# Both heads in one DRAM transfer, copies made by the fetch, and a block sum spread over the first pair: a change to a two-layer hybrid decoder trunk

## The chip, the cores and the metric

The kernel runs on one core of one Trainium2 chip. Its time is the device time of one execution in microseconds (us). The median of three runs of the kernel before is 2662.35 us (2662.26 to 2664.25). A core has five engines that run side by side, each with its own in-order stream of instructions: TensorE (PE, matrix products; the load of its weights is shown as PEld), VectorE (DVE), ScalarE (ACT), GpSimd (POOL) and SyncE (SP). In this kernel SP computes nothing: nearly all DMA transfers are issued from its queue, one after the other, and a transfer whose condition is not met holds back all that are queued behind it.

## The reference, cut to what matters

The input has 1024 tokens with 1024 features. There are two layers, each a pair of attention mixers with gates and then a gated convolutional FFN:

```python
h = rmsnorm(x, norm1[l])
proj = h @ w_in[l]                       # q, k, v of both mixers and the gates
o_a = dilated_mixture(qa, ka, va)        # 3 groups x 4 heads: windows 128/512/2048, dilation 1/4/16
o_b = stick_breaking_attention(qb, kb, vb)   # 4 heads
g_a, g_b = sigmoid gates of proj
x = x + (g_a * (o_a @ w_br[l, :OUT_A]) + g_b * (o_b @ w_br[l, OUT_A:])) @ w_o[l]
h2 = rmsnorm(x, norm2[l])
a, v = h2 @ w_up[l]
x = x + (gelu(causal_depthwise_conv(a)) * v) @ w_down[l]
```

A head has 64 features. The result must have float32 accuracy: the kernel writes every operand of a product as a rounded high part plus a low part and sums three matrix products (high by high, low by high, high by low), so that each product costs three passes of PE.

## The kernel before, in words

**Products in seven instead of eight.** The large projections go in *pairs*: two column blocks of 128 of `w_in` by the two halves of the tokens and the two halves of the features, a 2x2 block product that is done with seven block products instead of eight (`pair`, L1055). The price is in sums of blocks of the weights (L1077, L1078 on POOL, then on DVE) and of blocks of `h`. The four sums of `h` are called S[1] to S[4]; each has four parts of 128 features. They are made by `block_sums` (L984) in small pieces that stand in the list `dense.side`; the last is `fourth` (L1010): per part three additions of 128x512 on DVE (L1014 to L1016), then `split` (L136), that is, one copy on ACT for the high part and one subtraction on DVE for the low part. S[4] is written in place over the first block of `h` and is read by the seventh product of a pair alone.

**The order of PE.** PE's order is written by hand. The class `Dense` (L220) hands out the dense work in small steps; one step is six matrix products of 128x512 or so. First come four *plain* products (gates, L1211), then the pairs. `attend` (L361) walks over the attention items and asks for dense steps between their small pieces with `advance`; each call also does one piece of `dense.side`. When the first pair is to begin, what is left of `dense.side` is done at once (L310 to L315). `dense.at(n, f)` does `f` n steps later. The order on ACT, DVE, POOL and SP is set by a scheduler from the order of the program and the priorities in it.

**The items of a layer.** B0 to B15 are stick-breaking items (`stick_item`), N00 to N11 the near group of the dilated mixer (window 128, `near_item`, with ACT exponentials at L774 and the application of the weights at L796), T00 to T17 the two far groups together (`far_item`). A far item is one head pair `pr`, one head `s` of the pair and one remainder `r` of four. Pairs that are needed by an item come before it: `pair_near` for keys and queries of the stick-breaking and near heads, `pair_v` for values, `pair_kq` for keys and queries of the far groups (one pair for each group and head pair: four in a layer).

**The way through DRAM.** Results of these pairs go through DRAM to change their layout. A pair has four results (column block c, token half n); `put` writes each.

- `pair_kq.put` (L1139) writes keys and queries to `tk`. The high part of a key goes to rows 0 to 63 and the low part to rows 64 to 127; the high part of a query is written twice, to both row halves, and its low part once. Each of these is written for each of the two heads of the pair by a transfer of its own: 4 for a key block and 6 for a query block, 20 for a pair, each 64 rows by 4 remainders by 128 columns (L1148). The quarter that stays zero is written once by `zeros` (L1046) in the first layer.
- `fetch_kq` (L835) reads for one far item all six blocks of 128 rows by 256 with one transfer, into a new buffer (tag `xa`, four buffers for everything of that tag).
- `values_part` (L545) writes the values of the first four heads to `sv`, one transfer for a head (L566). `pair_v`'s `turn` (L1172) writes all other values, one transfer for each of two heads (L1186). The tiles hold the heads inside a token row (`j h c`, `r h c`).
- `fetch_row`, `fetch_values`, `fetch_whole` and `fetch_v` read stick-breaking and near keys, queries and values; they write into `slots` and `kv`.

The weights of the pairs come from `in_w_in_dram` (L1069), two transfers for a pair, on the same queue.

Of the kernel before, what the change touches and what calls it, by code (L numbers as in the profile page):

```python
# [7 lines left out]
F32 = mybir.dt.float32  # L8
# [54 lines left out]
def trunk_kernel(ctx, tc, x, norm1, w_in, b_gate, w_br, w_o, norm2, w_up, conv_w, conv_b, w_down, norm_f, out, depth=None, probe=None):  # L63
# [52 lines left out]
    tk = [dr.tile([2, 4, P, 6, 256], F32, name=f"tk{i}") for i in range(2)]  # L116
# [3 lines left out]
    sv = [dr.tile([P, KD, P], F32, name=f"sv{i}") for i in range(8)]  # L120
# [99 lines left out]
    class Dense:  # L220
# [324 lines left out]
    def values_part(vt, w, ms):  # L545
        for m in ms:
# [12 lines left out]
            ov = o.rearrange("p (j h c) -> p j h c", j=2, h=4)  # L559
            vv = vt[m // 2][:, 2 * (m % 2) : 2 * (m % 2) + 2, :, :]  # L560
# [95 lines left out]
    def fetch_values(j):  # L656
        u, qp = j // 4, 3 - j % 4
        t = slice(256 * qp, 256 * qp + 256)
        nc.sync.dma_start(f32(R["kv"][:, 1, t]).rearrange("p (b c) -> p b c", c=P), sv[u][:, 2 * qp : 2 * qp + 2, :])

    def fetch_whole(v):
# [6 lines left out]
        nc.sync.dma_start(f32(kv[:, 1, :]).rearrange("p (b c) -> p b c", c=P), sv[4 + v])  # L668
# [166 lines left out]
    def fetch_kq(i):  # L835

        t = R["kq", i] = sb.tile([P, 6, 256], F32R, tag="xa", bufs=4, name="t_kq")
        nc.sync.dma_start(f32(t), tk[i // 8][i // 4 % 2, i % 4])
# [5 lines left out]
    def far_item(dense, pr, s, r, share):  # L844
# [8 lines left out]
        def score():  # L853
# [7 lines left out]
            t = R["kq", i]  # L861
            for g in range(2):
                scores(z0[:, P * g : P * g + P], t[:, 3 * g + 1, 0:P], t[:, 3 * g + 2, 0:P], t[:, 3 * g, 0:P])
            for g in range(2):
                scores(z1[:, 256 * g : 256 * g + 256], t[:, 3 * g + 1, P:256], t[:, 3 * g + 2, P:256], t[:, 3 * g, :])
# [118 lines left out]
    def block_sums(more):  # L984
# [56 lines left out]
        todo += more  # L1041
        for i in range(4):
            todo.append(({"plain"}, lambda i=i: fourth(i)))
        return todo

    def zeros():  # L1046

        none = sb.tile([P, 4, 256], F32, tag="ot", name="none")
        pool.memset(none[0:64], 0.0)
        for pr in range(2):  # L1050
            for g in range(2):
                for s in range(2):
                    nc.sync.dma_start(tk[pr][s, :, 64:128, 3 * g + 2, :].rearrange("r p c -> p r c"), none[0:64])
# [82 lines left out]
    def pair_kq(dense, l, g, pr):  # L1136
        off = 256 * g + P * pr

        def put(c, n, x, psum, room=None):  # L1139
# [4 lines left out]
            for s in range(2):  # L1144
                rows = slice(64 * s, 64 * s + 64)
                for src, kind, up in ((hv, c, 0), (hv, 1, 64), (lv, 2, 0)) if c else ((hv, 0, 0), (lv, 0, 64)):
                    there = tk[pr][s, :, up : up + 64, 3 * (g - 1) + kind, n * P : (n + 1) * P]
                    nc.sync.dma_start(there.rearrange("r p j -> p r j"), f32(src[rows]))  # L1148
# [20 lines left out]
    def pair_v(dense, l, g):  # L1169


        def turn(c, n, f):  # L1172
# [4 lines left out]
            vv = sb.tile([P, 4, 2, P], F32R, tag="ot", name="vv")  # L1177
            with tc.high_priority(offset=AHEAD):
                act.copy(vv[:, :, :, 0:64], tw)
                dve.tensor_tensor(vv[:, :, :, 64:128], tw, f32(vv[:, :, :, 0:64]), ALU.subtract)  # L1180
            for h in range(2):
                if g:
                    there = tv[c][h, :, :, g - 1, n * P : (n + 1) * P].rearrange("r p c -> p r c")
                else:
                    there = sv[4 + 2 * c + h][:, 4 * n : 4 * n + 4, :]
                nc.sync.dma_start(there, f32(vv[:, :, h, :]))  # L1186
# [46 lines left out]
    def mixer(l, pending):  # L1233
# [6 lines left out]
        dense.side = block_sums([(set(), zeros)] * (l == 0))  # L1240
# [850 lines left out]
```

## Time and profile before

| what | value |
|---|---|
| median of 3 runs | 2662.35 us |
| profiled execution, its time | 2664.07 us |
| profiled execution, its span | 2662.4 us |
| mean granted TensorE clock | 0.997 |
| PE busy | 2628.7 us, 99% of the span |
| DVE, ACT, POOL busy | 78%, 50%, 28% |
| DMA | 478.76 MB, 416103 packets, mean 180 GB/s |

The span runs from the first to the last instruction. PE is busy nearly always, so whatever shortens the kernel without taking work from PE must be in the hundredth of the span in which PE stands still, or in stretches in which PE runs with a reduced clock. Busy times of the other engines are averages over stages with different limits. A view of stretches gives for each stretch its length, then the busy time of PE, PEld, DVE, ACT and POOL in it (with the number of instructions), the granted clock as a share of the full one, the share of the 16 DMA engines that was busy and GB/s. A view of waits gives the engine and line that waited, what ended the wait, the us in total, how often, and the longest.

### The profile page before, as it was taken

To read this page: it belongs to the slowest core of one execution; us is meant where nothing else is said; L and a number is where in the kernel's file an instruction comes from. 1 tells how busy PE (TensorE), PEld (TensorE's weight loads), DVE (VectorE), ACT (ScalarE), POOL (GpSimd) and SP (SyncE) were. 2 spreads that over 40 slices of the span, in tenths; PEclk is the share of its full clock that TensorE was granted. 3 is DMA by queue.
4 is the path that set the end of the run, shared out by engine and by line. 5 is a ranking of instruction groups with operands and counts; after the bars stand their busy time and mean duration, and the time that the engine had idled before them with its cause. 6 is when DMAs were issued, how large, how long until landed. Compare 5 with 4: busy or idle time off the path is not lost.

```text
span 2662.4 us, 36856 instructions
## 1 busy us (share of the span) xinstructions
PE 2628.7 (99%) x12780; PEld 2195.4 (82%) x12780; DVE 2070.3 (78%) x3094; ACT 1338.6 (50%) x2488; POOL 733.9 (28%) x609
## 2 busy tenths in 40 slices
PE   9999999999999999999999999999999999999999
PEld 8788878888888888888888888788888888888888
DVE  5887867785888888897659777567958888898865
ACT  5555556564545554432435555565645455554225
POOL 5422201121233443321162221101321343344210
PEclk9999999999999999999999999999999999999999
DMA  8443578773243544588442445886632544446863
GB/s 262 140 140 113 159 195 234 239 262 103 80 150 135 174 141 157 221 320 320 154 156 97 140 135 157 203 246 223 229 101 71 180 140 152 148 168 248 334 247 119
DMA packets 416103, 478.76 MB, mean 180 GB/s; under 512 B 25652, under 2 KB 335276, under 8 KB 414124
## 3 DMA queue, kind: packets, MB, share of 16 engines
q1 hardware_dynamic: 415900, 476.39, 55.0%
q8 instruction: 101, 1.65, 0.3%
q14 instruction: 86, 0.70, 0.1%
q10 hardware_dynamic: 16, 0.00, 0.0%
HBM read 307.43 MB, written 168.89 MB: 179 GB/s over the span
## 4 chain that ended last, share of the span: by engine, by line
PE 80%; DVE 10%; DMA 4%; ACT 2%; issue 2%; SPq 1%; POOL 1%; DVEq 0%; ACTq 0%; POOLq 0%
PE u_a L978 5%; PE u_a L980 5%; PE u_a L979 5%; PE d_ps L1719 5%; PE d_ps L1721 4%; PE d_ps L1720 4%; PE i_a L978 4%; PE i_a L980 3%; PE i_a L979 3%; PE u_c L979 3%; PE u_c L980 3%; PE u_c L978 3%; PE o_ps L181 2%; PE o_ps L180 2%; PE o_ps L182 2%
## 5 line engine op out<-in xcount | busy, mean ns | idle before, releaser
L146 DVE TENSOR_TENSOR w_lo<-up_a,w_hi 128x512 fp32r<-128x512 f32 x240 | 237.4, 996 | 20.5 <-ACT w_hi L139 20.5
L139 ACT CAST w_hi<-up_a 128x512 fp32r<-128x512 f32 x240 | 149.3, 622 | 184.1 <-PE u_a L979 45.4
L1727 DVE TENSOR_TENSOR x<-x,d_ps 128x512 f32<-128x512 f32 (+1 forms) x228 | 152.0, 671 | 78.4 <-PE d_ps L1721 77.0
L1458 POOL TENSOR_TENSOR cv<-cv 128x512 f32<-128x512 f32 x88 | 132.3, 1516 | 249.6 <-DVE cv L1453 139.7
L139 ACT CAST w_hi<-in_a 128x512 fp32r<-128x512 f32 x192 | 119.2, 621 | 130.5 <-PE i_c L979 45.9
L146 DVE TENSOR_TENSOR w_lo<-in_a,w_hi 128x512 fp32r<-128x512 f32 x192 | 142.5, 742 | 38.7 <-ACT w_hi L139 32.4
L146 DVE TENSOR_TENSOR g<-cv,g 128x512 fp32r<-128x512 f32 x154 | 151.9, 988 | 5.2 <-ACT g L139 2.7
L1077 POOL TENSOR_TENSOR u<-in_a 128x512 f32<-128x512 f32 x32 | 45.7, 1428 | 364.2 <-DMA in_a<-in_w_in_dram 116.2
L1719 PE MATMUL d_ps<-gd_in,w_hi 128*128 128x512 f32 (+1 forms) x340 | 130.3, 383 | 1.4 <-ACT w_hi L139 0.6
L1721 PE MATMUL d_ps<-gd_in,w_lo 128*128 128x512 f32 (+1 forms) x340 | 129.8, 382 | 0.0
L1720 PE MATMUL d_ps<-gd_in,w_hi 128*128 128x512 f32 (+1 forms) x340 | 129.7, 382 | 0.0
L978 PE MATMUL u_a<-hh,w_hi 128*128 128x512 f32 x320 | 124.7, 390 | 0.8 <-DVE u L1609 0.8
L980 PE MATMUL u_a<-hh,w_lo 128*128 128x512 f32 x320 | 124.5, 389 | 0.0
L979 PE MATMUL u_a<-hl,w_hi 128*128 128x512 f32 x320 | 124.5, 389 | 0.0
L980 PE MATMUL u_a<-t_hi,w_lo 128*128 128x512 f32 x320 | 124.5, 389 | 0.0
L979 PE MATMUL u_a<-t_lo,w_hi 128*128 128x512 f32 x320 | 124.5, 389 | 0.0
L978 PE MATMUL u_a<-t_hi,w_hi 128*128 128x512 f32 x320 | 124.5, 389 | 0.0
L146 DVE TENSOR_TENSOR w_lo<-w_raw,w_hi 128x512 fp32r<-128x512 f32 x96 | 77.0, 804 | 58.6 <-ACT w_hi L139 51.7
L691 POOL TENSOR_SCALAR_AFFINE_SELECT beta<-beta 128x128 f32<-128x128 f32 x64 | 31.8, 497 | 306.3 <-ACT beta L687 306.3
L139 ACT CAST g<-cv 128x512 fp32r<-128x512 f32 x154 | 95.0, 617 | 40.1 <-POOL cv L1458 29.6
L1719 PE MATMUL d_ps<-gd_in,wd 128*128 128x512 f32 (+1 forms) x292 | 113.9, 390 | 0.0
L1721 PE MATMUL d_ps<-gd_in,wd 128*128 128x512 f32 (+1 forms) x292 | 112.8, 386 | 0.0
(395 smaller groups left out, 8651.1 us busy)
## 6 DMA issues: line engine op xcount, KB each, us to landing
gd<-g SPq DMA_DIRECT2D x154, 512.0 KB, 3.6
gd_in<-gd SPq DMA_DIRECT2D x154, 512.0 KB, 6.8
up_a<-in_w_up_dram SPq DMA_DIRECT2D x80, 512.0 KB, 5.6
in_a<-in_w_in_dram SPq DMA_DIRECT2D x64, 512.0 KB, 5.6
t_kq<-tk SPq DMA_DIRECT2D x32, 768.0 KB, 4.9
wd_raw<-in_w_down_dram SPq DMA_DIRECT2D x22, 1024.0 KB, 11.7
gin<-gs SPq DMA_DIRECT2D x32, 512.0 KB, 4.8
w_raw<-in_w_o_dram SPq DMA_DIRECT2D x64, 256.0 KB, 2.9
```

Of the source, the lines that this page charges most:

```text
L139: one = act.copy(hi, src)
L146: two = dve.tensor_tensor(lo, src, f32(hi), ALU.subtract)
L180: pe.matmul(o, lh, rh, start=(first and i == 0), stop=False, skip_group_check=share)
L181: pe.matmul(o, lh, rl, start=False, stop=False, skip_group_check=share)
L978: pe.matmul(o, w[0][:, c], rh, start=(first and i == 0), stop=False, skip_group_check=True)
L979: pe.matmul(o, w[0][:, c], rl, start=False, stop=False, skip_group_check=True)
L980: pe.matmul(o, w[1][:, c], rh, start=False, stop=(last and i == 3), skip_group_check=True)
L1458: return lambda: pool.tensor_tensor(dst, a, b, ALU.subtract)
L1719: pe.matmul(o[:, sub], wh[:, c], gh[:, sub], start=(i == 0 and k in (0, 4, 5)), stop=False, skip_group_check=True)
L1720: pe.matmul(o[:, sub], wh[:, c], gl[:, sub], start=False, stop=False, skip_group_check=True)
L1721: pe.matmul(o[:, sub], wl[:, c], gh[:, sub], start=False, stop=(i == m - 1), skip_group_check=True)
L1727: dve.tensor_tensor(x, x, o[:, sub], ALU.add)
```

## The change

The change has five parts.

1. Writes to `tk`: the tile becomes `[2 heads, 64 rows, 4 remainders, 2 groups, 4 kinds, 256]`, with the kinds low key, high key, high query, low query. Each part of a result is written once, for both heads by one transfer of 128 rows: 2 transfers for each result, 8 for a pair.
2. Fetch for a far item: two tiles that stay for the layer, used in turn. A fetch is three transfers: three kinds of both groups to rows 0 to 63, and, for each group, low key and high query to rows 64 to 127. The quarter of zeros is set in each of the two tiles by a POOL memset of 64 rows by 2 times 256 at the first use; `zeros` with its eight transfers goes.
3. Values of the first four heads: the tile holds heads outside tokens, and one transfer writes four heads.
4. Values of `pair_v`: likewise, one transfer for two heads. ACT and DVE write the tile in that layout; their counts and shapes stay.
5. The four parts of `fourth` leave `dense.side`. When the first pair begins, `begin` puts them 1, 3, 5 and 7 dense steps later.

```diff
-    tk = [dr.tile([2, 4, P, 6, 256], F32, name=f"tk{i}") for i in range(2)]
+    tk = [dr.tile([2, 64, 4, 2, 4, 256], F32, name=f"tk{i}") for i in range(2)]
...
-    sv = [dr.tile([P, KD, P], F32, name=f"sv{i}") for i in range(8)]
+    sv = [dr.tile([P, n, KD, P], F32, name=f"sv{n}") for n in (4, 2, 2)]
...
                         self.started = True
+                        self.begin()
...
-            vv = vt[m // 2][:, 2 * (m % 2) : 2 * (m % 2) + 2, :, :]
+            vv = vt[m // 2][:, :, 2 * (m % 2) : 2 * (m % 2) + 2, :]
...
             if m % 2:
-                for u in range(4):
-                    nc.sync.dma_start(sv[u][:, 2 * m - 2 : 2 * m + 2, :], f32(vt[m // 2][:, :, u, :]))
+                nc.sync.dma_start(sv[0][:, :, 2 * m - 2 : 2 * m + 2, :], f32(vt[m // 2]))
...
     def fetch_kq(i):
 
-        t = R["kq", i] = sb.tile([P, 6, 256], F32R, tag="xa", bufs=4, name="t_kq")
-        nc.sync.dma_start(f32(t), tk[i // 8][i // 4 % 2, i % 4])
+        if i < 2:
+            t = R["kq", i] = sb.tile([P, 2, 3, 256], F32R, tag="xa", bufs=4, name="t_kq")
+            pool.memset(f32(t[64:128, :, 2, :]), 0.0)
+        t, there = R["kq", i % 2], tk[i // 8][i // 4 % 2, :, i % 4]
+        nc.sync.dma_start(f32(t[0:64]), there[:, :, 1:4, :])
+        for g in range(2):
+            nc.sync.dma_start(f32(t[64:128, g, 0:2, :]), there[:, g, 0:3:2, :])
...
-        todo += more
-        for i in range(4):
-            todo.append(({"plain"}, lambda i=i: fourth(i)))
-        return todo
-
-    def zeros():
-
-        none = sb.tile([P, 4, 256], F32, tag="ot", name="none")
-        pool.memset(none[0:64], 0.0)
-        for pr in range(2):
-            for g in range(2):
-                for s in range(2):
-                    nc.sync.dma_start(tk[pr][s, :, 64:128, 3 * g + 2, :].rearrange("r p c -> p r c"), none[0:64])
+
+        def begin():
+            for i in range(4):
+                dense.at(1 + 2 * i, lambda i=i: fourth(i))
+
+        return todo, begin
...
-            for s in range(2):
-                rows = slice(64 * s, 64 * s + 64)
-                for src, kind, up in ((hv, c, 0), (hv, 1, 64), (lv, 2, 0)) if c else ((hv, 0, 0), (lv, 0, 64)):
-                    there = tk[pr][s, :, up : up + 64, 3 * (g - 1) + kind, n * P : (n + 1) * P]
-                    nc.sync.dma_start(there.rearrange("r p j -> p r j"), f32(src[rows]))
+            for src, kind in ((hv, 1 + c), (lv, 3 * c)):
+                there = tk[pr][:, :, :, g - 1, kind, n * P : (n + 1) * P]
+                nc.sync.dma_start(there.rearrange("s p r j -> (s p) r j"), f32(src))
...
-            vv = sb.tile([P, 4, 2, P], F32R, tag="ot", name="vv")
+            vv = sb.tile([P, 2, 4, P], F32R, tag="ot", name="vv")
+            wv = vv.rearrange("p h r c -> p r h c")
...
-            for h in range(2):
-                if g:
-                    there = tv[c][h, :, :, g - 1, n * P : (n + 1) * P].rearrange("r p c -> p r c")
-                else:
-                    there = sv[4 + 2 * c + h][:, 4 * n : 4 * n + 4, :]
-                nc.sync.dma_start(there, f32(vv[:, :, h, :]))
+            if g:
+                there = tv[c][:, :, :, g - 1, n * P : (n + 1) * P].rearrange("h r p c -> p (h r) c")
+                nc.sync.dma_start(there, f32(vv).rearrange("p h r c -> p (h r) c"))
+            else:
+                nc.sync.dma_start(sv[1 + c][:, :, 4 * n : 4 * n + 4, :], f32(vv))
...
-        dense.side = block_sums([(set(), zeros)] * (l == 0))
+        dense.side, dense.begin = block_sums(dense)
```

Left out are the readers of `sv` (`fetch_values`, `fetch_whole`) and the indices of the score products in `far_item`, which follow the new layouts.

More of the change, by code (lines that the diff above doesn't have):

```diff
@@ L658, in fetch_values @@
         t = slice(256 * qp, 256 * qp + 256)
-        nc.sync.dma_start(f32(R["kv"][:, 1, t]).rearrange("p (b c) -> p b c", c=P), sv[u][:, 2 * qp : 2 * qp + 2, :])
+        nc.sync.dma_start(f32(R["kv"][:, 1, t]).rearrange("p (b c) -> p b c", c=P), sv[0][:, u, 2 * qp : 2 * qp + 2, :])
     def fetch_whole(v):
@@ L667, in fetch_whole @@
             nc.sync.dma_start(f32(R["slots"][up : up + 64, :, x, :]), q[x].rearrange("r (m c) -> r m c", c=256))
-        nc.sync.dma_start(f32(kv[:, 1, :]).rearrange("p (b c) -> p b c", c=P), sv[4 + v])
+        nc.sync.dma_start(f32(kv[:, 1, :]).rearrange("p (b c) -> p b c", c=P), sv[1 + v // 2][:, v % 2])
     def stick_item(dense, u, qp):
@@ L982, in seven, with block_sums @@
                 yield
-    def block_sums(more):
+    def block_sums(dense):
         last, rs = {}, {}
@@ L1176, in turn @@
             tw = tp.rearrange("p (r h c) -> p r h c", r=4, h=2)
-            vv = sb.tile([P, 4, 2, P], F32R, tag="ot", name="vv")
+            vv = sb.tile([P, 2, 4, P], F32R, tag="ot", name="vv")
+            wv = vv.rearrange("p h r c -> p r h c")
             with tc.high_priority(offset=AHEAD):
-                act.copy(vv[:, :, :, 0:64], tw)
-                dve.tensor_tensor(vv[:, :, :, 64:128], tw, f32(vv[:, :, :, 0:64]), ALU.subtract)
-            for h in range(2):
-                if g:
-                    there = tv[c][h, :, :, g - 1, n * P : (n + 1) * P].rearrange("r p c -> p r c")
-                else:
-                    there = sv[4 + 2 * c + h][:, 4 * n : 4 * n + 4, :]
-                nc.sync.dma_start(there, f32(vv[:, :, h, :]))
+                act.copy(wv[:, :, :, 0:64], tw)
+                dve.tensor_tensor(wv[:, :, :, 64:128], tw, f32(wv[:, :, :, 0:64]), ALU.subtract)
+            if g:
[3 more added lines that the diff above has]
+                nc.sync.dma_start(sv[1 + c][:, :, 4 * n : 4 * n + 4, :], f32(vv))
             if (c, n) == (1, 1):
```

8 lines of the change are left out of this document (4 added, 4 removed).

## The prediction, made before the changed kernel was run

> **What bounds the kernel now.** I read the page first, then the waits of PE, then short stretches around each wait, then the rows of the engines that ended it.
>
> ```profile
> span 2662.4 us, 36856 instructions
> PE 2628.7 (99%) x12780; PEld 2195.4 (82%) x12780; DVE 2070.3 (78%) x3094; ACT 1338.6 (50%) x2488; POOL 733.9 (28%) x609
> ```
>
> PE stands still for 2662.4 - 2628.7 = 33.7 us, 1.3% of the span. The change takes no matrix product away, so it can gain only from these 33.7 us and from stretches at a reduced clock. The waits of PE (us in total, times, longest) that lie in stages that the change touches:
>
> ```profile
> PE o L796 <- ACT p0h L139: 5.3, 3, 3.0
> PE z L621 <- DMA t_kq<-tk: 5.1, 5, 1.5
> PE i_c L978 <- ACT u L1100: 3.2, 2, 1.9
> PE z L622 <- DMA slots<-sq: 1.9, 3, 0.9
> ```
>
> That is 15.5 us. PE's order of time shows where the longest lie, and the stretches behind them what they cost afterwards:
>
> ```profile
> 132.27 0.50 PE L978 MATMUL i_c<-hh,w_hi 128*128 128x512 f32 x1 [1.92 <-ACT u L1100]
> 1446.83 0.50 PE L978 MATMUL i_c<-hh,w_hi 128*128 128x512 f32 x1 [1.28 <-ACT u L1100]
> 375.54 0.41 PE L796 MATMUL o<-p0h,kv 128*128 128x256 f32 x1 [2.03 <-ACT p0h L139]
> 1688.77 0.38 PE L796 MATMUL o<-p0h,kv 128*128 128x256 f32 x1 [2.98 <-ACT p0h L139]
> ```
>
> ```profile
> 132.00:136.00 4.00, 3.73 (x13) 3.05 (x14) 3.89 (x9) 2.29 (x5) 0.76 (x2) 0.68 0.00 0
> 136.00:140.00 4.00, 4.00 (x20) 3.33 (x20) 2.44 (x4) 1.68 (x3) 0.00 (x0) 0.90 0.27 87
> 376.00:380.00 4.00, 3.73 (x14) 3.12 (x15) 2.68 (x6) 1.01 (x2) 0.00 (x0) 0.60 0.76 187
> 1688.00:1692.00 4.00, 2.88 (x9) 2.32 (x10) 3.61 (x7) 2.21 (x6) 0.00 (x0) 0.74 0.72 171
> 1692.00:1696.00 4.00, 4.00 (x22) 3.38 (x22) 1.69 (x3) 1.62 (x3) 0.00 (x0) 0.84 0.37 91
> ```
>
> The granted clock (third number from the end) falls behind the three longest waits. What it costs is 4 us times the missing share: 4 x (0.32 + 0.10) = 1.7 us after 132, 4 x 0.40 = 1.6 us after 376, 4 x (0.26 + 0.16) = 1.7 us after 1688: 5.0 us in sum. The wait of 1.28 us has no such tail. So 15.5 + 5.0 = 20.5 us are within reach, if each wait has its cause in what is changed.
>
> The Trainium skill ("TensorE: Matmul & The Clock Gate", section "Why this matters for your kernels") asks for no PE gaps above about 3 us between bursts, since one idle window puts the clock to half. By that rule gaps of 2 us would be harmless and the dips would stay (rival D). The trace has three dips behind gaps of 1.92 to 2.98 us, so I keep them in the sum.
>
> **Part 5, the fourth sum (in reach 3.2 + 1.7 = 4.9 us).**
>
> ```profile
> L1014 DVE TENSOR_TENSOR h_sum<-hh,t_hi x8: 675/682/1777, 117.4 to 1440.9; 128x512 f32<-128x512 f32 x8
> 129.07 1.22 ACT L139 CAST hh<-h_sum 128x512 fp32r<-128x512 f32 x2 [2.93 <-DVE h_sum L1016]
> 131.63 0.60 ACT L1100 COPY u<-i_c 128x512 f32<-128x512 f32 x1
> ```
>
> In the first layer ACT stands 2.93 us before the copies of the fourth sum, since DVE has not finished the additions, and the copy that empties i_c (L1100) is queued behind. PE waits for that copy. The sum is four parts of four DVE operations of 0.68 us, 10.9 us of DVE, begun at 117.4. Spread at steps 1, 3, 5 and 7, the same 10.9 us are asked for over seven steps. The row at 136 counts 20 instructions of PE in 4 us, 0.2 us each; a step of six products with an attention piece of two to four beside it takes 1.6 to 2 us, so they spread over 11 to 14 us. DVE has its other work beside, so it stays nearly full, but only two of the four copies come before L1100. S[4] is read by the seventh product, which is past step 12, five steps after the last part. I take four fifths: 3.9 us. Ends: 4.9 us gained; 3.6 us lost (a wait of 1.92 with its tail of 1.7 once more, at the seventh product).
>
> **Part 1, the writes to tk (in reach 5.3 + 1.9 + 3.3 of tails = 10.5 us, and a share of the 5.1 us).** SP's rows (duration in ns, least/median/most; then rows in order of time):
>
> ```profile
> L1148 SPq DMA_DIRECT2D tk<-in_a x64: 574/611/1890, 340.1 to 1784.7; - x64
> ...
> DMA to landing us min/median/max: 2.4/2.5/5.5
> ...
> L1186 SPq DMA_DIRECT2D tv<-vv x32: 360/434/508, 321.4 to 1737.1; - x32
> 340.12 0.63 SPq L1148 DMA_DIRECT2D tk<-in_a  x1
> 356.38 0.62 SPq L1148 DMA_DIRECT2D tk<-u  x1
> 359.71 1.00 SPq L1069 DMA_DIRECT2D in_a<-in_w_in_dram  x2
> 1671.32 1.97 SPq L1069 DMA_DIRECT2D in_a<-in_w_in_dram  x2
> ```
>
> A pair issues 20 writes of 0.61 us, 12.2 us of SP; from 340 to 357 the queue does little else, and the next weights (in_a) go out only at 359.71. The nearest row for the new write, 128 rows by 4 by 128, is tv<-vv with 0.43 us: 8 x 0.43 = 3.5 us. SP gains up to 8.7 us a pair; some of it is time in which SP would wait for the results anyway, so I count on 5 us. Who waits for in_a:
>
> ```profile
> 369.06 1.30 POOL L1077 TENSOR_TENSOR u<-in_a 128x512 f32<-128x512 f32 x1 [38.16 <-DVE w_lo L146]
> 371.76 0.62 ACT L139 CAST w_hi<-in_a 128x512 fp32r<-128x512 f32 x1 [2.87 <-POOL in_a L1078]
> 1682.29 1.30 POOL L1077 TENSOR_TENSOR u<-in_a 128x512 f32<-128x512 f32 x1 [38.54 <-DMA in_a<-in_w_in_dram]
> 1685.00 0.62 ACT L139 CAST w_hi<-in_a 128x512 fp32r<-128x512 f32 x1 [3.82 <-POOL in_a L1078]
> ```
>
> POOL's block sums start as the weights come, ACT waits 2.87 and 3.82 us for them with the exponentials and the copies of a near item queued behind, and PE then waits 2.03 and 2.98 us at L796. In the first layer the row names DVE, which works on another tile there; I read it as in_a too. Weights that come 3.8 us sooner end both waits; 5 us are on offer. slots<-sq is behind the same writes. Late next would be ACT itself, which has the exponentials of a whole near item to do there. I take three quarters: 7.9 us. Ends: 10.5 us, and nothing (if the transfer and not its issue is what is late).
>
> **Part 2, the fetch (in reach 5.1 us).** It takes 64 partitions three times in place of 128 once:
>
> ```profile
> t_kq<-tk SPq DMA_DIRECT2D x32, 768.0 KB, 4.9
> L838 SPq DMA_DIRECT2D t_kq<-tk x32: 319/352/1852, 415.3 to 1842.2; - x32
> 396.95 1.86 SPq L667 DMA_DIRECT2D slots<-sq  x3
> 1672.92 9.21 DMA in_a<-in_w_in_dram
> 1791.23 7.66 DMA t_kq<-tk
> 487.06 0.32 SPq L838 DMA_DIRECT2D t_kq<-tk  x1
> 499.28 0.22 PE L621 MATMUL z<-t_kq 128*128 128x128 f32 x1
> ```
>
> The row of three (slots, rows 0 to 63, 64 to 127 and 0 to 63) is the nearest: 1.86 us against 0.35, so a fetch is out of the queue 1.5 us later. 32 fetches add 48 us of SP; 8 pairs give back up to 8 x 8.7 = 70 us. In the steady part this is covered: a fetch issued at 487.06 is first read at 499.28, 12.2 us later, and lands in 4.9 us, so 7.3 us are left. Without that cover each of the 32 would cost 1.5 us, 48 us in all. The five waits lie where fetches land in over 7 us (the chain that ended last holds one, at 1791.23), right behind the bursts of writes and weights. There the fetch loses 1.5 us, but it and the weights ahead of it go out up to 8.7 us sooner, and the bytes ahead of it fall: a pair writes 8 x 256 KB in place of 20 x 128 KB, 0.5 MB less, and a fetch reads 640 KB for 768. The waits are 1.0 us each on average. I take three quarters: 3.8 us. Ends: 5.1 us gained; 7.5 us lost (five times 1.5, if the bursts do not shrink).
>
> ```profile
> L1053 SPq DMA_DIRECT2D tk<-none x8: 615/664/1113, 81.0 to 96.3; - x8
> L648 POOL MEMSET slots<- x2: 947/948/949, 44.6 to 1357.3; 64x1024 f32 x2
> 414.60 1.29 POOL L1077 TENSOR_TENSOR u<-in_a 128x512 f32<-128x512 f32 x1 [12.47 <-DMA in_a<-in_w_in_dram]
> 415.30 0.33 SPq L838 DMA_DIRECT2D t_kq<-tk  x1
> ```
>
> The zeros leave SP (8 x 0.66 = 5.3 us) and POOL (one memset) around 81 to 96, where PE has none of the four waits: nothing gained. The four new memsets have half the elements of the one in the row, about 0.5 us each. Each waits on POOL for a buffer of tag xa to come free, with the block sums L1077 of the next weights behind it. The transfer at 415.30 waits for the same buffer, and L1077 ran at 414.60, so in that place the sums come about 0.7 + 0.5 = 1.2 us later. At the worst that is 1.2 us of PE in each layer; I count 0.6 us for both together, since most such delays end before PE needs the weights.
>
> **Parts 3 and 4, the values.** sv<-vb goes from 16 transfers to 4, the others from 48 to 24, with the same bytes. None of the four waits is on them; the writes of ACT and DVE keep their counts and shapes. No row shows the permuted write. At twice the 0.68 us of an addition of that size, 32 operations would add 22 us to DVE, on no listed wait of PE; cheaper, it would gain PE as little. I take zero.
>
> The sum: 3.9 + 7.9 + 3.8 - 0.6 = 15.0 us. The profiled execution took 2664.07 us, 1.7 us more than its span and than the median of 2662.35. On its own time it gives 2664.07 - 15.0 = 2649.1; I forecast 2649, which on the median is a gain of 13 us, half a per cent.
>
> **Rivals.**
>
> *A: the transfer engines are what is late, not the queue.* For it: in_a took 9.21 us from issue to its end and the fetches over 7, so earlier issue meets engines still full. Against: bytes fall, and zeros cost nothing now. Then part 5 comes as forecast (3.9), a third of the 10.5 and none of the 5.1: 2664.1 - 3.9 - 3.5 + 0.6 = 2657, and 2661 if the third fails too. The Trainium skill ("DMA: Bandwidth & Descriptors", section "Issuing engines are not separate DMA queues") says that the sequencer's time to start a transfer is usually small against the transfer, which is this rival; here 0.61 us stand against a landing of 2.5, but 20 stand in a row. Its section "Rules for kernel authors" advises one transfer of 128 partitions over two of disjoint halves, which speaks for the new writes and against the new fetch.
>
> *B: the waits move.* PE finds the next thing late: DVE in the first pair, ACT at the near items, the memset. Each of the three places gives back what it gained: 2664 - 2 = 2662, no change to be measured. For it: DVE is busy 3.89 of 4.00 us at 132, and half of the waits are ACT's.
>
> *C: slower.* If the new writes, which now lie between one another in one tile of DRAM, are taken for overlapping, each waits for the landing of the one before. Eight at 0.43 + 2.5 us of landing are 23 us in place of 12.2; all behind is 11 us later. The near items of the two layers wait already and have no cover: 2664 + 2 x 11 = 2686. It decides from the point where a burst is longer than 12.2 us. Against: the writes of before are as interleaved and go out 0.6 us apart, and the three into slots are done in 1.86 us.
>
> *D: the dips stay* though the waits go. Of the 5.0 us of dips the sum takes four fifths of 1.7 and three quarters of 3.3, 3.9 us: 2649 + 4 = 2653.
>
> **Chances.** Forecast (most waits end) 0.52; A 0.18; B 0.13; C or another lateness of that size 0.10; D 0.07. Measured against no change, 0.2% (5.3 us) is about what can be told. The forecast and D are faster, A mostly (0.16 of 0.18), B is the same, C slower: faster 0.75, same 0.15, slower 0.10. The forecast's own range is 2641 (all 20.5 us, and a little that the list leaves out) to 2656. The range goes to 2661, into B: it leaves out C, the slower half of B and 2 or 3 in a hundred below.
>
> **What will show it.** Right: no wait at L978 for L1100 in the first pairs and a clock of 1.00 after 132; L1148 with 64 issues below 0.5 us; L1077 three us or more sooner after the first near items, no wait of 2 us at L796, no dip at 376 and 1690; fetches beside the bursts landing in time. Wrong: L1148 at 0.6 us or with gaps of landings, a POOL memset ahead of a late L1077, or PE waiting for the seventh product.

## The result, and the profile after

The changed kernel took 2642.03 us (median of 4 runs, 2641.44 to 2642.24), the kernel before 2662.32 us beside it. The ratio is 0.9922, with a 95% interval of 0.9905 to 0.9939: 20.3 us less. The forecast was 2649 us; the range that the prediction gives goes from 2641, all that it saw in reach, to 2661.

The first lines of the page of the changed kernel:

```profile
span 2640.1 us, 36792 instructions
PE 2621.5 (99%) x12780; PEld 2192.0 (83%) x12780; DVE 2068.6 (78%) x3094; ACT 1337.7 (51%) x2488; POOL 734.9 (28%) x612
```

PE stands still for 2640.1 - 2621.5 = 18.6 us, where it was 33.7. The same 12780 products also take 7.2 us less (2628.7 before). The prediction put 5.0 us on the three falls of the clock; where the other 2.2 us come from was not followed. 15.1 + 7.2 = 22.3 us is the whole difference of the spans. Of that, 1.7 us is what the profiled execution of before stood above its median.

The waits of PE in the changed kernel (us in total, times, longest), from the top:

```profile
PE z L621 <- ACT stay L688: 2.7, 5, 1.1
PE warm L1979 <- POOL ident masks.py:199: 1.8, 1, 1.8
PE d_ps L1715 <- ACT w_hi L139: 1.4, 2, 1.1
...
PE o L796 <- DVE p0l L146: 0.6, 2, 0.3
...
PE o L796 <- ACT p0h L139: 0.3, 1, 0.3
```

Three of the four waits that the prediction listed (L1100, `t_kq`, `slots`) are gone from the list, and L796 is left with 0.3 us. Of the waits shown two have grown: L621 behind ACT's L688 was one wait of 1.2 us before, and L1715, in the FFN, had 0.6 us. The stretches at the three places where the clock fell (132, 369 and 1674), and one that comes later in the first pair (144):

```profile
132.00:136.00 4.00, 4.00 (x23) 3.33 (x22) 4.00 (x8) 1.62 (x3) 0.00 (x0) 1.00 0.17 49
144.00:148.00 4.00, 3.46 (x16) 2.49 (x14) 4.00 (x8) 3.01 (x7) 0.87 (x2) 1.00 0.32 112
369.00:373.00 4.00, 4.00 (x22) 3.23 (x22) 3.56 (x8) 1.94 (x5) 0.00 (x0) 1.00 1.06 247
1674.00:1678.00 4.00, 3.78 (x20) 3.00 (x19) 3.56 (x8) 2.19 (x6) 0.00 (x0) 1.00 0.96 256
```

The clock (third number from the end) is 1.00 in all of them. PE does the same instructions in the same order in every kernel of this document, so the start of one product can be compared with the start of the same product in another trace. These rows answer to the five PE rows of the prediction, which started at 132.27, 375.54, 499.28, 1446.83 and 1688.77:

```profile
130.07 0.40 PE L983 MATMUL i_c<-hh,w_hi 128*128 128x512 f32 x1
369.04 0.28 PE L796 MATMUL o<-p0h,kv 128*128 128x256 f32 x1
487.55 0.22 PE L621 MATMUL z<-t_kq 128*128 128x128 f32 x1
1434.46 0.47 PE L983 MATMUL i_c<-hh,w_hi 128*128 128x512 f32 x1
1673.97 0.28 PE L796 MATMUL o<-p0h,kv 128*128 128x256 f32 x1
```

They lead by 2.2, 6.5, 11.7, 12.4 and 14.8 us. Taking the same difference for every product gives the gain by stretch (the time is that of the trace before):

| stretch, us | what lies there | gain, us |
|---|---|---|
| 0 to 160 | fourth sum, first layer | 2.3 |
| 160 to 360 | | 0.6 |
| 360 to 400 | first near item and its clock dip | 6.1 |
| 400 to 440 | next near items | -0.8 |
| 440 to 520 | first far items | 3.5 |
| 520 to 1400 | rest of the layer | -1.3 |
| 1400 to 1480 | fourth sum, second layer | 0.35 |
| 1480 to 1680 | | 0.9 |
| 1680 to 1760 | near items | 6.7 |
| 1760 to 1800 | far items | 2.8 |
| 1800 to the end | | 1.25 |

The near and far items hold 6.1 + 3.5 + 6.7 + 2.8 = 19.1 us of 22.4. The table sets one execution against one. The kernel with parts 3 and 4 alone (below), whose median shows no change, leads by 1.1 us in the stretch 0 to 160 and by 4.1 us in 1680 to 1760 in its own trace, so the gains of these two stretches are uncertain by as much; in the other three stretches of the near and far items it moves by less than 0.1 us.

SP's rows for the new transfers (duration in ns, least/median/most), then SP and POOL in order of time:

```profile
L1144 SPq DMA_DIRECT2D tk<-in_a x24: 512/546/1338, 337.6 to 1757.7; - x24
L841 SPq DMA_DIRECT2D t_kq<-tk x32: 573/580/856, 408.4 to 1821.0; - x32
L843 SPq DMA_DIRECT2D t_kq<-tk x64: 573/598/1654, 409.0 to 1822.3; - x64
```

```profile
349.72 1.29 SPq L1067 DMA_DIRECT2D in_a<-in_w_in_dram  x2
358.52 1.33 POOL L1075 TENSOR_TENSOR u<-in_a 128x512 f32<-128x512 f32 x1 [30.55 <-ACT u L1102]
```

Before, the weights went out at 359.71 and POOL's block sum started at 369.06. Both are some 10 us sooner, of which 2.9 us are the lead that PE has by then (2.3 + 0.6 in the table): against the products beside them the weights come 7.1 us sooner. In the second layer they go out at 1654.85 and not at 1671.32, 16.5 us sooner with a lead of 10.9, that is 5.6 us. The sums are done at 361.2 (L1076 ends them), and ACT's long row of exponentials of the near item begins at 364.20. In the row shown, what ends POOL's wait before the block sum is now a copy of ACT (L1102), no longer the weights.

### The profile page after: what moved, and what is told of

It reads as the page before. It is cut to its first block, busy times and chain, and to the rows that moved or that the text cites. A ratio compares the mean times of both kernels' runs of the same rounds, so it can differ in the third digit from the quotient of the medians.

```text
span 2640.1 us, 36792 instructions
## 1 busy us (share of the span) xinstructions
PE 2621.5 (99%) x12780; PEld 2192.0 (83%) x12780; DVE 2068.6 (78%) x3094; ACT 1337.7 (51%) x2488; POOL 734.9 (28%) x612
## 4 chain that ended last, share of the span: by engine, by line
PE 83%; DVE 9%; issue 3%; DMA 2%; ACT 2%; POOL 1%; SPq 0%; DVEq 0%; POOLq 0%; ACTq 0%
PE u_a L983 5%; PE u_a L985 5%; PE u_a L984 5%; PE d_ps L1715 5%; PE d_ps L1716 5%; PE d_ps L1717 5%; PE i_a L983 4%; PE i_a L985 4%; PE i_a L984 4%; PE u_c L985 3%; PE u_c L983 3%; PE u_c L984 3%; PE o_ps L180 2%; PE o_ps L181 2%; PE o_ps L182 2%
## 5 line engine op out<-in xcount | busy, mean ns | idle before, releaser
L1715 PE MATMUL d_ps<-gd_in,w_hi 128*128 128x512 f32 (+1 forms) x340 | 130.3, 383 | 2.3 <-ACT w_hi L139 1.4
L983 PE MATMUL u_a<-hh,w_hi 128*128 128x512 f32 x320 | 124.7, 390 | 0.4 <-DVE u L1605 0.3
L983 PE MATMUL u_a<-t_hi,w_hi 128*128 128x512 f32 x320 | 124.5, 389 | 0.0
L1715 PE MATMUL d_ps<-gd_in,wd 128*128 128x512 f32 (+1 forms) x292 | 113.9, 390 | 0.0
```

The lines of the kernel that those rows point to most:

```text
L983: pe.matmul(o, w[0][:, c], rh, start=(first and i == 0), stop=False, skip_group_check=True)
L1715: pe.matmul(o[:, sub], wh[:, c], gh[:, sub], start=(i == 0 and k in (0, 4, 5)), stop=False, skip_group_check=True)
```

## The experiments

**The three groups of parts, each alone on the kernel before.** The theory was that the gain lies in the queue of SP, with parts 1 and 2; the rivals were that part 5, or the values, bring a good part of it.

The fourth sum alone (part 5):

```diff
                         self.started = True
+                        self.begin()
...
-        for i in range(4):
-            todo.append(({"plain"}, lambda i=i: fourth(i)))
-        return todo
+        def begin():
+            for i in range(4):
+                dense.at(1 + 2 * i, lambda i=i: fourth(i))
+        return todo, begin
```

> The kernel before with part 5 alone (the fourth sum at steps 1, 3, 5, 7 of the first pair; zeros stays). My theory: the waits of PE at L978 for the copy L1100 and the clock dip after 132 us go, and nothing else: 3.2 + 1.7 = 4.9 us less, 2657 to 2658 us, with the waits at L796 (5.3 us) and their dips at 376 and 1688 us still there. Rival (the waits move): the seventh product of the first pair or the next copy waits instead, 2661 to 2663 us.

2659.41 us against 2661.43, ratio 0.9996 (0.9987 to 1.0005): not told from no change. Waits of PE in this kernel:

```profile
PE z L622 <- DMA t_kq<-tk: 5.0, 5, 1.7
PE o L797 <- ACT p0h L139: 3.7, 2, 2.1
PE z L622 <- ACT stay L689: 2.8, 5, 1.2
```

The wait for L1100 is gone, so the spread does what it says. The waits of the near and far items stay. The wait behind ACT's L689 (L688 before) grows from 1.2 us in one place to 2.8 us in five: that is a price of part 5.

`tk` alone (parts 1 and 2; the edit is the change's own for `tk`, `fetch_kq`, `far_item`, `zeros` and `pair_kq.put`):

> The kernel before with parts 1 and 2 alone (writes to tk for both heads, copies by the fetch, zeros gone). My theory: the waits at L796, for slots and for t_kq go with two dips, 5.3 + 1.9 + 5.1 + 3.3 = 15.6 us: 2646 to 2648 us; the first pairs keep 1.9 and 1.3 us at L1100 and the dip after 132. Rival (the three transfers of a fetch cost what the writes give): 2655 us or more, with waits for t_kq left.

2642.34 us, ratio 0.9929 (0.9915 to 0.9942): 19.1 us less than the 2661.43 beside it, nearly the whole of the change. Its largest wait of PE, and the stretch behind it:

```profile
PE i_c L983 <- ACT u L1096: 2.6, 2, 1.3
```

```profile
132.48 0.50 PE L983 MATMUL i_c<-hh,w_hi 128*128 128x512 f32 x1 [1.31 <-ACT u L1096]
```

```profile
131.00:135.00 4.00, 2.69 (x14) 2.13 (x14) 3.96 (x10) 3.30 (x8) 0.88 (x2) 1.00 0.14 48
```

The wait that part 5 removes is still there, at 1.31 us in the first layer instead of 1.92, and with no fall of the clock behind it. So with parts 1 and 2 there is less left for part 5 to gain than the 4.9 us in reach before. Why the wait is shorter was not tested. One difference is `zeros`, which goes with part 2: the fetch alone (below), also without it, has the same 1.31 us there, while the values alone, which keep it, have 1.71. The prediction put the leaving of `zeros` at nothing gained.

The values alone (parts 3 and 4; the edit is the change's own for `sv`, `vv` and their readers):

> The kernel before with parts 3 and 4 alone (values of four heads and of two heads by one transfer). My theory: no wait of PE hangs on these writes, 2661 to 2663 us. Rival: the shorter queue alone helps the near items, since the values of a pair are written in the same stretch; 2656 to 2660 us with a shorter wait at L796.

2661.99 us, ratio 1.0003 (0.9995 to 1.0012). The waits are those of before:

```profile
PE o L795 <- ACT p0h L139: 5.5, 2, 3.8
PE z L620 <- DMA t_kq<-tk: 5.0, 5, 1.9
PE i_c L977 <- ACT u L1099: 3.0, 2, 1.7
```

The three groups add to 2.0 + 19.1 - 0.6 = 20.5 us, and the change gave 20.3: the groups do not help or hinder each other by more than these runs can tell.

**The queue or the transfer engines?** Three kernels change the number of issues and not the bytes, or the bytes and not the number, on the changed kernel. First, 12 transfers of 64 rows by 16 bytes for each pair, from the results to scratch in DRAM, so that a pair issues 20 again:

```diff
             for src, kind in ((hv, 1 + c), (lv, 3 * c)):
                 there = tk[pr][:, :, :, g - 1, kind, n * P : (n + 1) * P]
                 nc.sync.dma_start(there.rearrange("s p r j -> (s p) r j"), f32(src))
+                for more in range(1 + c):
+                    nc.sync.dma_start(idle[l, g - 1, pr, c, n, 2 * (kind in (0, 3)) + more], f32(src[0:64, 0, 0:4]))
```

> The changed kernel with 12 short transfers more for each pair of keys and queries (64 rows of 16 bytes, into DRAM that nobody reads), issued behind the two writes of each result, so that a pair has 20 issues again while its bytes stay those of the changed kernel. Theory 'the queue is what was late': the queue gets back some 12 x 0.6 = 7 us a pair, the weights go out late again and waits at L796 or for slots and t_kq come back: 2647 to 2653 us. Theory 'the transfer engines were late' (rival A): fewer and larger packets were what helped, 2641 to 2643 us, PE's waits as in the changed kernel.

2681.76 us, ratio to the kernel before 1.0076 (1.0063 to 1.0088): 39.7 us above the changed kernel, with 0.1 MB more moved. The direction is that of the queue theory, but the loss is far above the 2647 to 2653 us expected. The longest wait of PE, the added transfers, and the weights and that wait in order of time:

```profile
PE z L622 <- DMA t_kq<-tk: 15.4, 8, 4.1
```

```profile
L1147 SPq DMA_DIRECT2D idle<-in_a x32: 588/631/1905, 338.4 to 1798.2; - x32
```

```profile
356.70 1.17 SPq L1068 DMA_DIRECT2D in_a<-in_w_in_dram  x2
483.32 0.44 PE L622 MATMUL z<-t_kq 128*128 128x128 f32 x1 [4.12 <-DMA t_kq<-tk]
```

A transfer of 1 KB holds the queue for 0.63 us, as long as one of 128 KB. The fetches wait behind them.

Next, four such transfers for a pair, that is, 12 issues:

```diff
+            nc.sync.dma_start(idle[l, g - 1, pr, c, n], f32(lv[0:64, 0, 0:4]))
```

> The changed kernel with 4 short transfers more for each pair of keys and queries (one behind each result), 12 issues a pair. With 12 more the time rose by 39 us, 4.9 us a pair. If the loss is in proportion to the issues, 4 more cost 13 us: 2654 to 2657 us. If the burst has cover and only a longer one reaches PE, 2641 to 2645 us.

2649.02 us, ratio 0.9954 (0.9942 to 0.9967): 7 us above the changed kernel. A third of the issues costs about a sixth of the time, so the price is not one per issue. Only 1.8 us of the loss lie at the far items; 4.7 us lie between 1680 and 1760. There PE waits for DVE's `vv` (3.0 us in all, longest 1.7), DVE for ACT's copy into that tile, and ACT for an earlier write `tv<-vv` to land (13.6 us in eight places, 7.3 us in five in the changed kernel). So a longer queue also costs by way of the values' writes, not only by late fetches; which of the issues in front makes these writes late was not followed.

The other way round, the copies are made by the writes as before, but for both heads at once: 10 writes of 256 KB for a pair, the zeros by four transfers, and a fetch of 128 rows and 768 KB in one transfer:

```diff
-    tk = [dr.tile([2, 64, 4, 2, 4, 256], F32, name=f"tk{i}") for i in range(2)]
+    tk = [dr.tile([2, 64, 2, 4, 6, 256], F32, name=f"tk{i}") for i in range(2)]
...
+        t = R["kq", i % 2] = sb.tile([P, 2, 3, 256], F32R, tag="xa", bufs=4, name="t_kq")
+        nc.sync.dma_start(f32(t).rearrange("p g k c -> p (g k c)"), tk[i // 8][i // 4 % 2, :, :, i % 4].rearrange("p u k c -> (p u) (k c)"))
...
-            for src, kind in ((hv, 1 + c), (lv, 3 * c)):
-                there = tk[pr][:, :, :, g - 1, kind, n * P : (n + 1) * P]
+            for src, kind, up in ((hv, 1, 0), (hv, 1, 1), (lv, 2, 0)) if c else ((hv, 0, 0), (lv, 0, 1)):
+                there = tk[pr][:, :, up, :, 3 * (g - 1) + kind, n * P : (n + 1) * P]
```

> The changed kernel with part 2 undone in another way: the copies are again made by the writes, but each write serves both heads (10 for a pair, 256 KB each, the bytes of the kernel before), the rows of the two halves lie alternately so that a fetch is one transfer of 128 rows and 768 KB, and the zeros are written once by 4 transfers. Theory 'the number of issues in the burst decides': 10 issues of 0.55 us are 5.5 us a pair against 4.4, and the fetch saves 1.2 us each; 2641 to 2643 us, as the changed kernel. Theory 'bytes and packets decide' (rival A): the bytes are those of before, so waits for t_kq and at L796 come back; 2648 us or more.

2645.35 us against 2661.02 beside it, ratio 0.9939 (0.9925 to 0.9952). It moves the bytes of the kernel before (478.72 MB against 478.76), and has 15.7 of the 20 us:

```profile
DMA packets 401892, 478.72 MB, mean 181 GB/s; under 512 B 23732, under 2 KB 316972, under 8 KB 399916
```

```profile
L1149 SPq DMA_DIRECT2D tk<-in_a x32: 359/369/766, 336.6 to 1760.1; - x32
L838 SPq DMA_DIRECT2D t_kq<-tk x32: 319/336/1238, 408.6 to 1823.4; - x32
```

No wait for `t_kq` is left in it, and its first near item gains 6.1 us as in the changed kernel. It stands 3.3 us above the changed kernel, which the two intervals do not separate; its list of waits has 1.9 us for DVE's `vv` where the changed kernel's has 0.7, and 1.1 us for `p1l` where that has 0.4. The place is again 1680 to 1760, where it gains 3.5 us and the changed kernel 6.7, and again ACT's copy into `vv` waits for `tv<-vv` to land (11.8 us in eight places). Whether its larger transfers cause this was not tried.

**Part 2 by itself.** The fetch in three transfers into two tiles that stay, and `zeros` gone, with the 20 writes and the layout of the kernel before:

```diff
-        t = R["kq", i] = sb.tile([P, 6, 256], F32R, tag="xa", bufs=4, name="t_kq")
-        nc.sync.dma_start(f32(t), tk[i // 8][i // 4 % 2, i % 4])
+        if i < 2:
+            t = R["kq", i] = sb.tile([P, 6, 256], F32R, tag="xa", bufs=4, name="t_kq")
+            pool.memset(f32(t[64:128].rearrange("p (g k) c -> p g k c", k=3)[:, :, 2, :]), 0.0)
+        t, there = R["kq", i % 2], tk[i // 8][i // 4 % 2, i % 4]
+        nc.sync.dma_start(f32(t[0:64]), there[0:64])
+        for g in range(2):
+            nc.sync.dma_start(f32(t[64:128, 3 * g : 3 * g + 2, :]), there[64:128, 3 * g : 3 * g + 2, :])
```

> The kernel before with the fetch of part 2 alone: 20 writes for a pair as before, three transfers for a fetch, two tiles that stay, zeros by memset. Theory 'issues decide': the fetch adds about 1.5 us each where the bursts leave no cover, and the short transfers behind full bursts gave 20 us over before with idle issues; 2670 to 2682 us, with waits for t_kq of 10 us or more. Theory 'bytes decide': a fetch reads 640 KB in place of 768 and the zeros are gone; 2658 to 2663 us.

2674.68 us, ratio 1.0054 (1.0042 to 1.0067): 13.7 us slower than before. Its waits of PE, then rows in order of time:

```profile
PE z L621 <- issue: 7.0, 2, 3.6
PE o L796 <- ACT p0h L139: 6.1, 3, 3.1
PE z L621 <- DMA t_kq<-tk: 3.8, 5, 1.5
```

```profile
366.56 1.29 POOL L1073 TENSOR_TENSOR u<-in_a 128x512 f32<-128x512 f32 x1 [38.19 <-DMA tk<-in_a]
373.03 0.38 PE L796 MATMUL o<-p0h,kv 128*128 128x256 f32 x1 [3.11 <-ACT p0h L139]
461.36 0.57 SPq L841 DMA_DIRECT2D t_kq<-tk  x1
471.74 1.26 SPq L843 DMA_DIRECT2D t_kq<-tk  x2
474.57 0.45 PE L621 MATMUL z<-t_kq 128*128 128x128 f32 x1 [3.42 <-issue]
1688.65 1.30 POOL L1073 TENSOR_TENSOR u<-in_a 128x512 f32<-128x512 f32 x1 [38.41 <-DVE st L773]
1695.11 0.38 PE L796 MATMUL o<-p0h,kv 128*128 128x256 f32 x1 [2.73 <-ACT p0h L139]
```

A fetch in three transfers can be torn: its first part went out at 461.36, the other two at 471.74. Between them stand six writes to `tk` in the queue, and the first of these held it from 461.9 to 467.8, since the result that it writes was not there yet. PE waits 3.42 us at 474.57, and the clock then falls (0.50 and 0.65 in the next two stretches of 4 us). The view calls this wait "issue" and names no transfer; that it is the late part of the fetch follows from the order of time alone. The same comes at 1798, with the parts at 1788.94 and 1795.62. Part 2 alone is a loss; together with part 1 the loss is not seen.

These rows also settle what holds the near item. In the kernel before, the block sum starts at 369.06 and 1682.29, and PE's L796 6.48 us later, at 375.54 and 1688.77. Here it starts at 366.56 and 1688.65, and L796 comes 6.47 and 6.46 us later. In the changed kernel the sum is at 358.52, L796 at 369.04, 10.5 us later and without a wait: the sum no longer sets it.

The queue's load puts these kernels in order. For a pair (and the four fetches that fall to it), issues times their durations:

| kernel | writes and added transfers, us | with 4 fetches, us | waits for `t_kq`, us | time, us |
|---|---|---|---|---|
| copies by 10 writes | 4.1 | 5.4 | none | 2645.4 |
| changed | 4.3 | 11.4 | none | 2642.0 |
| changed, 4 transfers more | 7.1 | 14.2 | 0.9 | 2649.0 |
| before | 12.2 | 13.6 | 5.1 | 2662.3 |
| changed, 12 transfers more | 11.9 | 19.0 | 15.4 | 2681.8 |
| fetch alone | 12.3 | 18.9 | 3.8, and 7.0 as "issue" | 2674.7 |

In these runs a queue of 11 us a pair costs no more than one of 5; at 19 the time is 30 to 40 us above the changed kernel's. Between them it matters where the load lies: before and the kernel with four transfers more have nearly the same sum, but the burst of writes ahead of the near item is 12.2 us in the one and 7.1 in the other.

**What the fourth sum still costs.** First, the sum left out:

```diff
         def begin():
-            for i in range(4):
-                dense.at(1 + 2 * i, lambda i=i: fourth(i))
+            S[4] = half(0, 0)
```

> The changed kernel with the fourth sum left out altogether (the seventh product of each pair reads the block of h itself). It bounds what part 5 can bring. Theory 'DVE's work is what PE meets later': the half us and the 1.1 us that PE gives back some 10 and 20 us after the spread sums (a wait for L688 at the scores) go too; 2637 to 2640 us. Theory 'the scores were early anyway': they wait for ACT whether the sum is made or not; 2641 to 2643 us and the wait for L688 of some 2.7 us stays.

2639.02 us, ratio 0.9919 (0.9906 to 0.9931). That is 3.0 us below the changed kernel by the medians and 3.6 by the spans (2636.5 against 2640.1), with intervals that overlap. L621 waits for L688 in one place only:

```profile
PE z L621 <- ACT stay L688: 1.1, 1, 1.1
```

Four of its five places in the changed kernel thus come with the fourth sum. These are two of the four, one in each layer, in the changed kernel:

```profile
134.10 0.63 ACT L139 CAST hh<-h_sum 128x512 fp32r<-128x512 f32 x1 [2.67 <-DVE h_sum L1021]
147.61 0.50 PE L621 MATMUL z<-kv,slots 128*128 128x512 f32 x1 [0.54 <-ACT stay L688]
1452.10 0.51 PE L621 MATMUL z<-kv,slots 128*128 128x512 f32 x1 [0.58 <-ACT stay L688]
```

Then three other places for it on the changed kernel: steps 1, 4, 7, 10; one of the three additions of a part on POOL; steps 3, 5, 7, 9.

```diff
-                dense.at(1 + 2 * i, lambda i=i: fourth(i))
+                dense.at(1 + 3 * i, lambda i=i: fourth(i))
```

> The changed kernel with the four parts of the fourth sum 1, 4, 7 and 10 dense steps after the pair begins, in place of 1, 3, 5 and 7. The changed kernel waits 2.7 us in five places at L621 for ACT's L688, and leaving the fourth sum out altogether gave 2639.0 against 2642.0. If those waits come from DVE and ACT being asked for the sum too densely, the wider spread takes them away, about 2640 and L688 below 1.5 us. If what DVE gives up at one place it lacks at another, it stays within 1 us of 2642; if the last part comes too late for the seventh product, PE waits there for a copy or a subtraction of the sum, 2643 to 2646.

```diff
-            dve.tensor_tensor(r, f32(ah), f32(S[2][i][0]), ALU.subtract)
+            pool.tensor_tensor(r, f32(ah), f32(S[2][i][0]), ALU.subtract)
```

> The changed kernel with the first of the three additions of each part of the fourth sum on POOL in place of DVE, at the same steps. DVE loses 4 x 0.68 = 2.7 us of work in the first pair, POOL gets 4 x about 1.3 us. If DVE's fullness is what the waits behind L688 come from, about 2640. If POOL, which has the block sums of the weights in the same stretch, is late, 2643 to 2646, with waits for POOL's additions or for L1077 and its copies.

```diff
-                dense.at(1 + 2 * i, lambda i=i: fourth(i))
+                dense.at(3 + 2 * i, lambda i=i: fourth(i))
```

> The changed kernel with the four parts of the fourth sum at steps 3, 5, 7 and 9, as dense as in the changed kernel but two steps later. If the density alone makes the waits behind L688, they move by two steps and stay, 2642. If the place decides, because an item with its own work on ACT and DVE lies at steps 5 to 7, the waits change in size by over 1 us, up or down, 2640 or 2644.

Beside 2661.45 us of the kernel before they took 2641.16 (0.9920, 0.9907 to 0.9934), 2651.03 (0.9959, 0.9947 to 0.9972) and 2642.47 us (0.9930, 0.9917 to 0.9942). A row of the wider spread:

```profile
1455.14 0.44 PE L716 MATMUL sb_t<-ident,beta 128*128 128x128 f32 x2 [1.79 <-DVE beta L708]
```

The wider spread and the later place both take away the waits behind L688 (1.2 and 0.7 us left) and put a wait for DVE at L716 in their place, 1.79 us in each layer in the one, 2.15 and 2.27 us in the other. What DVE gives up at one place it lacks at another, and the times do not differ from the changed kernel's by more than the runs can tell. No version here beats it clearly. POOL is the wrong place for an addition: PE then waits 3.19 and 3.58 us at L983 for a copy of ACT (L1093) that is queued behind the copies of the sum, and the clock falls to 0.58 in the stretch from 131 to 135. Its 2651 us lie outside both times expected; ACT stands 7.91 us before the first of these copies, and POOL does its addition only behind the block sums of the weights.

## Why the prediction was right, point by point

**The bound, 20.5 us in reach.** Right: 22.3 us of span went (20.3 us by the medians), which is about all of it. The forecast's discount, 15.0 of 20.5, was what made 2649 of 2642.

**Part 1, 7.9 of 10.5 us.** The mechanism held: `in_a` out sooner, block sum sooner, no wait at L796, no dip. The term was too small. The near items gained 6.1 and 6.7 us, of which 0.8 was given back, so about 12 in these two traces, and the far items' 6.3 us belong to this part too (next point). The "5 us" of SP was about right: against the products beside them the weights came 7.1 and 5.6 us sooner, more than the 3.8 us that the prediction needed to end both waits. The step that fell short is the three quarters taken of that for ACT being late next: L796 was left with 0.3 us behind ACT. The price of a write was wrong in the other sense, 0.54 us and not 0.43, so that "64 issues below 0.5 us", named as a sign of being right, did not come; 8 x 0.11 = 0.9 us a pair was too little to matter.

**Part 2, 3.8 of 5.1 us.** The waits for `t_kq` went, and the far items gained 3.5 + 2.8 = 6.3 us. But the sum credits this to the wrong part. The kernel with 10 writes and a fetch of one transfer, as before, has no such waits either (3.5 and 2.8 us gained at the same places), and the new fetch alone loses 13.7 us. It was the shorter burst of writes. The forecast's price of the fetch was right (1.78 us against 0.35, 1.4 us more, forecast 1.5), and its bound of "7.5 us lost, if the bursts do not shrink" was too mild: a torn fetch costs a wait of over 3 us (3.42 and 3.60) and a clock dip.

**Part 5, 3.9 of 4.9 us.** Too large. The stretches of the fourth sum gained 2.3 and 0.35 us, but `tk` alone, without part 5, gains 1.4 and 0.0 us in the same stretches. By itself part 5 brought 2.0 us with an interval that holds zero; beside parts 1 and 2 the medians leave it 0.3 us (2642.34 against 2642.03). The step that failed is the four fifths. DVE "stays nearly full", as the prediction said: it is busy 4.00 of 4.00 us from 132 to 136 and again from 144 to 148. So the lateness moved to the next stick-breaking item, where ACT's L688 is late for PE's L621. That is rival B at this one place: without the sum the span is 3.6 us shorter still, though the intervals of the times overlap. The named sign, PE waiting for the seventh product, did not come.

**The memsets, -0.6.** Not seen. The 0.8 us given back between 400 and 440 might have been theirs, but the kernel with 10 writes, which has no memset of a fetched tile, gives back 0.95 us at the same place.

**Parts 3 and 4, zero.** Right, 1.0003 (0.9995 to 1.0012).

**What was luck.** Parts 1 and 2 brought 19.1 us where the sum had 7.9 + 3.8 - 0.6 = 11.1, and part 5 brought 2.0 us by itself and 0.3 beside them where it had 3.9. The two misses pull in opposite directions, and the time came out close to the lower end of the range; had part 5 brought its 3.9 us on top of parts 1 and 2, it would have been below 2641. The mechanism that carried the forecast, a burst of issues on SP ahead of the weights and the fetches, is the one that the runs show.

**The rivals.** A, the transfer engines: refuted as the main cause by two kernels, one with the issues back and no bytes, one with the bytes back and few issues. A third agrees: the fetch alone moves 6.3 MB less than the kernel before in more issues, and is slower. The Trainium skill ("DMA: Bandwidth & Descriptors", section "Issuing engines are not separate DMA queues") calls the time to start a transfer usually small against the transfer. Of a single one that holds here (0.55 us against a landing of 3), but not of 20 in a row, which hold the queue for 12.2 us ahead of a fetch. C, writes that wait for each other's landing: not seen, the last writes of the first burst are 0.7 us apart. D, dips without waits: refuted, the clock is 1.00 at all three places.

## What to carry to other kernels

Add up issue times, not bytes, for a queue that carries both bursts of small writes and fetches with a deadline: here 12 issues more for a pair cost 40 us and 4 more cost 7, with next to no bytes. A transfer that must be in time can be torn when it is split, as here between writes that stood waiting for their data, so test such parts of a change alone. When a piece of work is spread on an engine that is full, look at the next item of that engine for the lateness; by taking the work out altogether one run shows how much is left to be gained.

## What the runs showed of the hardware that was not expected

**Where the clock falls.** In these traces every single gap of PE of 1.92 us or more was followed by a fall of the clock, and the gaps of 1.28, 1.31 and 1.79 us named above were not. Two of them lie at the same product, in the wider spread behind 1.79 us at 1455.14 and in the later place behind 2.27 us at 1456.18:

```profile
1455.00:1459.00 4.00, 3.86 (x20) 3.27 (x21) 2.96 (x5) 1.76 (x4) 0.95 (x1) 1.00 0.73 209
```

```profile
1456.00:1460.00 4.00, 3.82 (x11) 3.05 (x12) 2.96 (x5) 1.00 (x2) 0.64 (x1) 0.58 0.83 213
```

But the length of one gap is not the whole rule. In the fourth sum alone the clock falls behind a gap of 1.68 us, and in the values alone it stays behind one of 1.89 us:

```profile
1687.99 0.38 PE L797 MATMUL o<-p0h,kv 128*128 128x256 f32 x1 [1.68 <-ACT p0h L139]
1688.00:1692.00 4.00, 3.66 (x12) 2.77 (x13) 3.13 (x6) 1.46 (x3) 0.00 (x0) 0.65 0.80 188
```

```profile
1788.44 0.30 PE L620 MATMUL z<-t_kq 128*128 128x128 f32 x1 [1.89 <-DMA t_kq<-tk]
1788.00:1792.00 4.00, 3.56 (x23) 3.29 (x24) 1.89 (x6) 2.43 (x7) 0.00 (x0) 1.00 1.15 334
```

In the fetch alone even a gap of 1.17 us, at 455.40, has a fall behind it (0.61 from 456 to 460). PE stands still a second time close to that one (0.38 us) and to the one of 1.68 us (0.34 us), so what else is idle nearby may count; these runs do not settle it. With the tail of 1.6 to 1.7 us that the prediction worked out, a gap of 2 us cost nearly 4 us here. The Trainium skill ("TensorE: Matmul & The Clock Gate", section "Why this matters for your kernels") sets its limit at about 3 us; the measurement decides, and in these traces the clock fell behind shorter gaps.

**What an issue costs.** In these runs it does not follow the bytes: 0.63 us for 64 rows of 16 bytes, 0.61 for 64 rows of 2 KB, 0.54 for 128 rows of 2 KB into the layout of the change, and 0.37 for most of the same 128 rows into that of the kernel with 10 writes. What sets it, and why the last two differ, stays open.
